# Two weight units ahead of the first norm, the squares of x behind them, and 10 idle products instead of 14

## The chip, the cores and the metric

The kernel runs on one core of a Trainium2 chip. The metric is the device time of one execution in microseconds (us). Three runs of the kernel before took 877.97, 880.21 and 880.77 us, so the median is 880.21 us.

## The reference, cut to what matters

One layer of a hybrid trunk on x of shape (1, 512, 1024), in float32. An RMS norm of x feeds one wide projection; its columns go to four token mixers (gated DeltaNet, RG-LRU, S5, RWKV-7) and to four gates; the gated branches are summed, projected and added to x, and a squared-ReLU MLP and a last norm follow.

```python
h = _rmsnorm(x, norm1_g)        # x * rsqrt(mean(x*x) + EPS) * g
proj = h @ w_in
p_gdn, p_lru, p_s5, p_rwkv, p_gate = _split(proj, ...)
ys = (gdn(p_gdn), rglru(p_lru), s5(p_s5), rwkv7(p_rwkv))
merged = sum(sigmoid(gate_i) * (ys[i] @ w_branch[i]))
x = x + merged @ w_out
x = x + square(relu(_rmsnorm(x, norm2_g) @ mlp_w1)) @ mlp_w2
```

## The kernel before, in words

Everything is held transposed: channels on the 128 partitions, the 512 tokens along the free axis. x comes as eight tiles `xs[0..7]` of 128x512 (L251).

**Units.** The weights come as 134 units of 128x1024 floats. `unit` (L316) asks for one: a DMA into one of four `raw` buffers (L313), on ACT a copy that rounds it to the high part `hi` (through the helper `act`, L117), on DVE a subtraction that leaves the low part `lo` (through `tt`, L120). There are two pairs of hi/lo buffers, so the high part of unit n waits until TensorE (PE) has finished unit n-2. A product of a unit is 24 matmuls of 128x512 (`gemm`, L337: eight blocks k, and in each hi by high, hi by low, lo by high part of x); "products" below means such matmuls.

**The first norm.** `norm1` (L406) does two things. `split_g` (L382) makes the high part (ACT, L117) and low part (DVE, L129) of each x tile, scaled by the norm's weight. `norm_stat` (L345) squares each tile on ACT, adds the squares on DVE (L120), lets PE sum them over the partitions (tile `ssa`), takes root and reciprocal (`sta`), and spreads the result with four matmuls (`rsa`) into the row `rs`. The projection runs on the unscaled x, and each result is multiplied by `rs` afterwards (`nproj`, L419), so PE does not need `rs` to start, but no result of the projection leaves PSUM before it is there. The first six accumulators have a PSUM bank each (EARLY = 6).

**What sets the order.** The program is written step by step (PLAN, L68), but the instructions are put in order by a list scheduler: each has a priority (`unit` gives -50000 to unit 0 and 100*u - 30000 to unit u, steps get levels by LV), and among those that its own timeline takes to be ready, the one of the best priority goes next on its engine. An engine then runs its list strictly in order. A change at the start shifts what is ready when, and so the order of everything in the mixers behind it.

**The triangular solve.** `tri_inverse` (L442), run for RWKV ("r") and for DeltaNet ("g"), is a chain over all engines: DMAs through a DRAM scratch (`scrr`, `scrg`; L446, L450), fifteen small steps on DVE, DMAs back and forth again (L466, L470), then bursts of tiny matmuls `zp` (128), `t1p` (192), `z2p` and `z3p` (64 each), with copies on ACT and DVE between them (L492, L507, L509, L519). "zpr" is the first burst for RWKV, "t1pr" the second, and so on; "zpg" that for DeltaNet.

**The S5 output.** `s5_y` (L1325) copies two PSUM tiles on ACT (L1335), writes them to DRAM (`scy`, L1338, from SP's queue), reads them back by 16 small DMAs issued from ACT's queue (L1344), adds on DVE (L129), applies Gelu on ACT, and multiplies by a weight on PE (`glu`).

The idle products are matmuls of a column of ones at the very start (`warm`, WARM of them; each is two instructions on PE).

Of the kernel before, what the change touches and what calls it, by code (L numbers as in the profile page):

```python
# [11 lines left out]
ACT = mybir.ActivationFunctionType  # L12
# [39 lines left out]
    sqc2=c3:236 sqc3=c3:16 sqc4=c3:533 sqc5=c3:610 sqc6=c3:562 sqc7=c3:594 rsc=c3:0  # L52
""".split())}
NU = 134
WARM = 14
EARLY = 6
GRAN = 32
DEEP = 2
# [39 lines left out]
RW0 = 1800  # L98
GATE0 = 2824
@with_exitstack  # L100
def trunk(ctx, tc, order, xT, wall, w8, prm, big, cst, gfr, out):
    nc = tc.nc
    V, A, G, P = nc.vector, nc.scalar, nc.gpsimd, nc.tensor
# [9 lines left out]
    def mm(o, l, r, start=True, stop=True):  # L113
        P.matmul(out=o, lhsT=l, rhs=r, start=start, stop=stop)  # L114

    def act(o, i, f, scale=1.0, bias=0.0):
        A.activation(out=o, in_=i, func=f, scale=scale, bias=bias)  # L117

    def tt(e, o, a, b, op):
        e.tensor_tensor(out=o, in0=a, in1=b, op=op)  # L120
# [44 lines left out]
    def fr(*ts_):  # L165
        clock[0] += 1
        for t in ts_:
            _, r, o, g, nm = live.pop(id(t))
            regions[r][1][o:o + g] = False
            regions[r][2][o:o + g] = clock[0]  # L170
# [10 lines left out]
    def t2(name, dt=F, where=None):  # L181
        return al(name, 512, dt, where)
# [10 lines left out]
    @contextmanager  # L193
    def priority(n):
        old = tc.cur_priority
        tc.cur_priority = n
        yield
        tc.cur_priority = old
# [14 lines left out]
    def ps(name):  # L213
        t = bank[0]
        turn[t] = (turn.get(t, -1) + 1) % BANKS[t]
        return pmx.tile([128, 512], F, tag=f"{t}{turn[t]}", name=name)
# [3 lines left out]
    def pa(name):  # L220

        n = turn["acc"] = turn.get("acc", -1) + 1
        if n < EARLY or turn.get("late"):
            b = n % 6
            if b >= 3:
                return pmx.tile([128, 512], F, tag=("g0", "g1", "s0")[b - 3], name=name)
            return pacc.tile([128, 512], F, tag=f"acc{b}", name=name)
        return pacc.tile([128, 512], F, tag=f"acc{n % 3}", name=name)


    def v3(t, a):
        return t.rearrange("p (a b) -> p a b", a=a)
# [4 lines left out]
    def bc(ap, shape):  # L237
        return ap.to_broadcast(shape)
# [7 lines left out]
    xs = [v3(xt, 8)[:, k] for k in range(8)]  # L246
# [44 lines left out]
    with priority(-70000):  # L291
        o = ps("warm")
        for i in range(WARM):
            mm(o[:, 0:128], ones, ones)
# [4 lines left out]


    count = {"u": 0, "raw": 0}
    third = []

    def place(key):
        if key not in order:
            order.append(key)
        return order.index(key)

    def load(key):
        n = count["raw"]  # L310
        count["raw"] += 1
        raw = wp.tile([128, 1024], F, tag=f"raw{n % NRAW}", name=f"raw{n}")
        nc.sync.dma_start(out=raw, in_=wall[place(key)])  # L313
        return raw

    def unit(key, more=None, chain=None):  # L316

        u = count["u"]
        count["u"] += 1
        with priority(100 * u - (30000 if u else 50000)):  # L320
            k = u % (DEEP + len(third) // 2)
            if k < DEEP:
                hi, lo = (wp.tile([128, 1024], R, tag=f"{e}{k}", name=f"{e}{u}") for e in ("hi", "lo"))
            else:
                hi, lo = third
            if chain is None:
                raw = load(key)
            else:
                raw = chain
                (G if more is None else nc.sync).dma_start(out=raw, in_=wall[place(key)], **({"accum_op": ADD} if more is None else {}))  # L330
            if more is not None:
                G.dma_start(out=raw, in_=wall[place(more)], accum_op=ADD)
            act(hi, raw, ACT.Copy)
            tt(V, lo, raw, hi.bitcast(F), SUB)
        return v3(hi, 8), v3(lo, 8)

    def gemm(o, w, rh, rl, nk=8, k0=0, first=True, last=True):  # L337
        wh, wl = w
        n = 0
        for k in range(nk):  # L340
            for a, b in ((wh, rh), (wh, rl), (wl, rh)):
                mm(o, a[:, k0 + k, :], b[:, k, :], first and n == 0, last and n == 3 * nk - 1)
                n += 1

    def norm_stat(xt, nm, parts=1):  # L345

        accs = []
        for k in range(8):
            sq = t2(f"sq{nm}{k}")
            act(sq, xt[k], ACT.Square)  # L350
            if k == 0 or k == 7:
                accs.append(sq)
            else:
                tt(V, accs[-1], accs[-1], sq, ADD)
                fr(sq)
        while len(accs) > parts:
            tt(V, accs[-2], accs[-2], accs[-1], ADD)
            fr(accs.pop())
        def keep_warm(n, t):
            if parts > 1:  # L360
                w = pa("warm")
                for _ in range(n):
                    mm(w[:, 0:128], ones, t[:, 0:128])

        o = ps("ss" + nm)
        for i, acc in enumerate(accs):
            for u in range(4):
                mm(o[:, u:u + 1], acc[:, u * 128:u * 128 + 128], one, i + u == 0, i == parts - 1 and u == 3)
            keep_warm(3, acc)
        fr(*accs)  # L370
        st = sm_.tile([128, 4], F, name="st" + nm)
        act(st, o[:, 0:4], ACT.Sqrt, 1.0 / 1024, eps_c)
        V.reciprocal(out=st, in_=st)
        rs = t2("rs" + nm)
        for h in range(2):
            o = ps("rs" + nm)
            for u in range(2):
                mm(o[:, u * 128:u * 128 + 128], bc(st[:, 2 * h + u:2 * h + u + 1], [128, 128]), ident)
            A.copy(out=rs[:, h * 256:h * 256 + 256], in_=o[:, 0:256])
        return rs  # L380

    def split_g(x, gname, k, hi, lo):  # L382

        act(hi, x, ACT.Copy, p(gname, k))
        stt(lo, x, p(gname, k), hi.bitcast(F), MUL, SUB)
# [17 lines left out]
    xgh, xgl = v3(xgh_, 8), v3(xgl_, 8)  # L403
    N1 = {}

    def norm1():  # L406

        for k in range(8):
            split_g(xs[k], "g1", k, xgh[:, k, :], xgl[:, k, :])
        N1["rs"] = norm_stat(xs, "a")  # L410
        fr(xt)

    def proj(col):

        o = pa("acc")
        gemm(o, unit(("in", col)), xgh, xgl)
        return o

    def nproj(t, col):  # L419
        tt(V, t, proj(col), N1["rs"], MUL)  # L420
        return t
# [851 lines left out]
    def s5_b():  # L1273
        b8 = S5["b8"]
        b83 = v3(b8, 16)

        up = t4("s5u")
        upv = up.rearrange("p (m t n) -> p m t n", m=2, t=8)
        scu = dram.tile([2, 128, 512], F, name="scu")
        for m in range(2):  # L1280
            tt(V, upv[:, m].rearrange("p t n -> p n t"), v3(proj(1544 + 128 * m), 64), v3(N1["rs"], 64), MUL)
            nc.sync.dma_start(out=scu[m], in_=up[:, m * 512:m * 512 + 512])
        ug = t4("s5ug")
        uf = scu.rearrange("m (g c) (t n) -> t c (m g) n", c=16, t=8)
        for t in range(8):
            nc.scalar.dma_start(out=v3(ug, 16)[16 * (7 - t):16 * (7 - t) + 16], in_=uf[t])
        ug3 = v3(ug, 16)
        H = t4("s5h")

        for r in range(2):  # L1290
            o = ps("s5v")
            for g in range(16):
                r0 = 64 * (g % 2)
                mm(o[r0:r0 + 64, (g // 2) * 64:(g // 2) * 64 + 64], b83[:, g, 64 * r:64 * r + 64], ug3[:, g, :])
            A.copy(out=H[:, 512 * r:512 * r + 512], in_=o)
        fr(b8)
        S5.update(up=up, ug=ug, H=H)
# [379 lines left out]
    def y_of(i, f):  # L1677
# [3 lines left out]

    steps = {
        "norm_a": norm1, "reg_y": lambda: region("c1a", 4096, R), "s5_a": s5_a, "s5_o": s5_o, "s5_b": s5_b, "s5_c": s5_c, "s5_y": y_of(2, s5_y), "lru_a": lru, "lru_g": y_of(1, lru_g),
        "rwkv_t": lambda: tri_prepare("r"), "rwkv_a": rwkv_a, "rwkv_b": rwkv_b, "rwkv_i": rwkv_i, "rwkv_r": rwkv_r, "rwkv_o": y_of(3, rwkv_o),
        "gdn_t": lambda: tri_prepare("g"), "gdn_k": lambda: gdn_a("k"), "gdn_v": lambda: gdn_a("v"), "gdn_q": lambda: gdn_a("q"), "gdn_l": gdn_logits, "gdn_b": gdn_b, "gdn_i": gdn_i, "gdn_r": gdn_r, "gdn_z": gdn_z, "gdn_c": y_of(0, gdn_c),
# [143 lines left out]
```

## Time and profile before

| | |
|---|---|
| median of three runs | 880.21 us |
| the profiled execution, its own time | 878.37 us |
| its span from first to last instruction | 876.6 us |
| PE busy | 852.6 us (97%) |
| DVE, ACT busy | 547.4 us, 427.2 us |
| mean granted TensorE clock | 0.988 |
| PE's idle time before 26 us | 0.89 at the very start, then some 3 us |
| PE's idle time from 150 to 335 us | some 12 us in 12 waits |
| PE's idle time from 350 to 800 us | 0.33 us |

PE is the engine that is nearly always busy. The first table of the page gives each engine's share of the span; the waits of PE, asked for by engine, say where the other 3% go; the timeline of the first 26 us shows the three engines step by step. "Busy" for PE includes the time in which it runs at half of its clock, which the granted clock of short windows shows.

### The profile page before, as it was taken

To read this page: it belongs to the slowest core of one execution; us is meant where nothing else is said; L and a number is where in the kernel's file an instruction comes from. 1 tells how busy PE (TensorE), PEld (TensorE's weight loads), DVE (VectorE), ACT (ScalarE), POOL (GpSimd) and SP (SyncE) were. 2 spreads that over 40 slices of the span, in tenths; PEclk is the share of its full clock that TensorE was granted. 3 is DMA by queue.
4 is the path that set the end of the run, shared out by engine and by line. 5 is a ranking of instruction groups with operands and counts; after the bars stand their busy time and mean duration, and the time that the engine had idled before them with its cause. 6 is when DMAs were issued, how large, how long until landed. Compare 5 with 4: busy or idle time off the path is not lost.

```text
span 876.6 us, 13021 instructions
## 1 busy us (share of the span) xinstructions
PE 852.6 (97%) x5175; PEld 683.9 (78%) x5175; DVE 547.4 (62%) x974; ACT 427.2 (49%) x600; POOL 26.0 (3%) x38
## 2 busy tenths in 40 slices
PE   8999999998999899999999999999999999999996
PEld 6777777777767677777888788888888888888885
DVE  6899796993676347845645652454437553868553
ACT  8735557954532254433523333765545443644433
POOL 1000000000000000000000000000100110010000
PEclk9999999998999899999999999999999999999998
DMA  8433345455365643344232232556676877463302
GB/s 298 134 114 104 109 117 111 105 148 147 111 182 155 163 144 111 107 119 136 73 106 99 75 130 96 192 145 174 164 195 165 239 170 194 164 137 104 120 25 96
DMA packets 79293, 119.97 MB, mean 137 GB/s; under 512 B 42544, under 2 KB 49392, under 8 KB 79216
## 3 DMA queue, kind: packets, MB, share of 16 engines
q1 hardware_dynamic: 51968, 100.40, 35.5%
q0 software_dynamic: 3456, 12.58, 8.5%
q10 hardware_dynamic: 23808, 6.16, 3.3%
q8 instruction: 40, 0.66, 0.3%
q14 instruction: 21, 0.17, 0.1%
HBM read 103.79 MB, written 13.17 MB: 133 GB/s over the span
## 4 chain that ended last, share of the span: by engine, by line
PE 80%; DVE 7%; DMA 6%; ACT 4%; issue 2%; ACTq 1%; SPq 1%; DVEq 0%
PE acc L114 24%; PE facc L114 20%; PE dacc L114 17%; PE oacc L114 5%; PE bacc L114 5%; DVE c L120 2%; DMA c1a<-scrg 1%; ACT c L117 1%; DVE lo L120 1%; PE s L114 1%; DVE c1a L120 1%; DVE c L129 1%; ACT L117 1%; DMA c1a<-gscr 1%; DMA scrg<-c1a 1%
## 5 line engine op out<-in xcount | busy, mean ns | idle before, releaser
L114 PE MATMUL acc<-c,hi 128*128 128x512 f32 x864 | 279.1, 401 | 3.1 <-DVE c L129 2.5
L117 ACT ACTIVATE hi<-raw 128x1024 fp32r<-128x1024 f32 x113 | 119.5, 1058 | 214.8 <-PE facc L114 73.5
L120 DVE TENSOR_TENSOR lo<-raw,hi 128x1024 fp32r<-128x1024 f32 x113 | 138.1, 1223 | 117.9 <-ACT hi L117 117.8
L114 PEld LDWEIGHTS acc<-c,hi 128*128 128x128 f32 x864 | 162.4, 191 | 43.2 <-DVE c L129 5.0
L114 PE MATMUL acc<-c,lo 128*128 128x512 f32 x432 | 175.1, 406 | 2.0 <-DVE lo L120 2.0
L114 PE MATMUL facc<-c,hi 128*128 128x512 f32 x336 | 103.4, 389 | 0.0
L114 PEld LDWEIGHTS acc<-c,lo 128*128 128x128 f32 x432 | 82.3, 190 | 21.9 <-DVE lo L120 3.1
L117 ACT ACTIVATE c<-c 128x512 f32<-128x512 f32 (+5 forms) x101 | 63.9, 638 | 19.3 <-DVE c L120 12.3
L114 PEld LDWEIGHTS facc<-c,hi 128*128 128x128 f32 x336 | 63.1, 188 | 13.0
L120 DVE TENSOR_TENSOR c<-c 128x16 f32<-128x16 f32 (+8 forms) x125 | 65.3, 537 | 5.1 <-ACT c L117 4.6
L114 PE MATMUL facc<-c,lo 128*128 128x512 f32 x168 | 65.5, 390 | 0.0
L114 PE MATMUL facc<-c,c1a 128*128 128x512 f32 x264 | 62.8, 391 | 0.0
L114 PE MATMUL dacc<-hi,c 128*128 128x512 f32 x176 | 57.4, 389 | 0.0
L117 ACT ACT_TABLE_LOAD x41 | 52.6, 1283 | 9.6 <-DMA c<-scu 3.7
L114 PEld LDWEIGHTS facc<-c,c1a 128*128 128x128 f32 x264 | 49.3, 188 | 10.2
L120 DVE TENSOR_TENSOR c1a<-raw,c1a 128x1024 fp32r<-128x1024 f32 x21 | 25.7, 1223 | 32.8 <-ACT c1a L117 32.7
L120 DVE TENSOR_TENSOR c<-acc,c 128x512 f32<-128x512 f32 x33 | 22.6, 688 | 36.3 <-PE acc L114 34.7
L114 PE MATMUL bacc<-c1a,hi 128*128 128x512 f32 x128 | 41.8, 408 | 0.3 <-DVE c L120 0.3
L117 ACT ACTIVATE c1a<-raw 128x1024 fp32r<-128x1024 f32 x21 | 22.2, 1059 | 36.6 <-PE facc L114 29.0
L114 PE MATMUL oacc<-c,hi 128*128 128x512 f32 x128 | 39.8, 392 | 0.1
L114 PEld LDWEIGHTS dacc<-hi,c 128*128 128x128 f32 x176 | 33.0, 188 | 6.9
L114 PEld LDWEIGHTS facc<-c,lo 128*128 128x128 f32 x168 | 31.5, 188 | 6.5
(394 smaller groups left out, 1187.2 us busy)
## 6 DMA issues: line engine op xcount, KB each, us to landing
raw<-in_wall_dram SPq DMA_DIRECT2D x134, 512.0 KB, 3.5
c<-in_wall_dram POOLq DMA_DIRECT2D x18, 512.0 KB, 5.8
c<-in_wall_dram SPq DMA_DIRECT2D x6, 512.0 KB, 3.5
raw<-in_wall_dram POOLq DMA_DIRECT2D x6, 512.0 KB, 6.2
scg<-c1b SPq DMA_DIRECT2D x11, 256.0 KB, 2.4
c<-scg SPq DMA_DIRECT2D x11, 256.0 KB, 4.2
c1b<-in_xT_dram SPq DMA_DIRECT2D x8, 256.0 KB, 5.4
c<-in_xT_dram SPq DMA_DIRECT2D x8, 256.0 KB, 4.8
```

The costliest lines, as they stand in the source:

```text
L114: P.matmul(out=o, lhsT=l, rhs=r, start=start, stop=stop)
L117: A.activation(out=o, in_=i, func=f, scale=scale, bias=bias)
L120: e.tensor_tensor(out=o, in0=a, in1=b, op=op)
L129: V.scalar_tensor_tensor(out=o, in0=a, scalar=s, in1=b, op0=op0, op1=op1)
```

## The change

The two first units of the projection (columns RW0 + 768 and RW0 + 896, which `rwkv_a` uses first) are asked for inside `norm1`, ahead of the splits, and kept in the list `early` until `proj` takes them. `unit` keeps the ACT instruction that makes each high part in the list `high`. All instructions of `norm_stat` on ACT are ordered behind `high[1]`, the high part of unit 1 (`tc.issue_after` adds an order edge on that instruction's engine alone). WARM goes from 14 to 10. The numbers of the units and their order in DRAM stay the same, and no work is added or left out but the four idle products.

```diff
-WARM = 14
+WARM = 10
...
-    third = []
+    third, high, early = [], [], []
...
-            act(hi, raw, ACT.Copy)
+            high.append(A.activation(out=hi, in_=raw, func=ACT.Copy, scale=1.0, bias=0.0).ins)
             tt(V, lo, raw, hi.bitcast(F), SUB)
...
     def norm1():
 
+        early.extend(unit(("in", RW0 + 128 * m)) for m in (6, 7))
         for k in range(8):
             split_g(xs[k], "g1", k, xgh[:, k, :], xgl[:, k, :])
-        N1["rs"] = norm_stat(xs, "a")
+        with tc.issue_after(high[1]):
+            N1["rs"] = norm_stat(xs, "a")
         fr(xt)
 
     def proj(col):
 
         o = pa("acc")
-        gemm(o, unit(("in", col)), xgh, xgl)
+        gemm(o, early.pop(0) if early else unit(("in", col)), xgh, xgl)
```

The order on ACT at the start. `c_75<-c1b,pr` is the high part of an x tile, `c_79<-c1b` (also c1a, c_78) its square, `hi_180`, `hi_214`, `hi_266` are the high parts of units 0, 1 and 2. Before, from the seventh x tile on (the six pairs ahead of these rows read the same):

```order
L117 ACTIVATE c_75<-c1b,pr 128x512
L117 ACTIVATE c_79<-c1b 128x512
L117 ACTIVATE c_75<-c1b,pr 128x512
L117 ACTIVATE c_78<-c1b 128x512
L117 ACTIVATE hi_214<-raw_216 128x1024
L117 ACTIVATE c_79<-cs,pr 128x128 x2
L117 ACTIVATE c_79<-pr 128x16
L117 ACTIVATE ea<-pr 128x4
L117 ACTIVATE cl<-pr 128x2
L117 ACTIVATE cl<-cl 128x2
L117 ACTIVATE hi_266<-raw_268 128x1024
```

Now, from the first instruction that works on data on, with units 0, 1, 2 as `hi_113`, `hi_119`, `hi_262`:

```order
L333 ACTIVATE hi_113<-raw_115 128x1024
L117 ACTIVATE c_75<-c1b,pr 128x512 x8
L333 ACTIVATE hi_119<-raw_121 128x1024
L117 ACTIVATE c_79<-c1b 128x512 x5
L117 ACTIVATE c1a<-c1b 128x512
L117 ACTIVATE c_79<-c1b 128x512
L117 ACTIVATE c_78<-c1b 128x512
L117 ACTIVATE c_79<-cs,pr 128x128 x2
L117 ACTIVATE c_79<-pr 128x16
L117 ACTIVATE ea<-pr 128x4
L117 ACTIVATE cl<-pr 128x2
L333 ACTIVATE hi_262<-raw_264 128x1024
```

The eight squares stood between the splits; they now stand in one block between the high parts of units 1 and 2. DVE follows: the low parts of x (L129) were alternating with the additions of squares (L120 of 128x512), and now come in one run of eight, then the low part of unit 1, then the additions.

The order on PE where the norm's sum over partitions (`ssa`) stands. Before, 26 products are ahead of it (24 of unit 0, two of unit 1):

```order
L114 MATMUL acc<-c_75,lo_181 128x512
L114 MATMUL ssa<-one,c_79 128x1 x4
L114 MATMUL acc<-c_75,hi_266 128x512 x2
L114 MATMUL acc<-c_75,lo_215 128x512
L114 MATMUL acc<-c_75,hi_214 128x512 x2
```

Now 50 products are ahead of it (units 0 and 1, two of unit 2):

```order
L114 MATMUL acc<-c_75,lo_120 128x512
L114 MATMUL acc<-c_75,hi_262 128x512 x2
L114 MATMUL ssa<-one,c_79 128x1 x4
L114 MATMUL acc<-c_75,hi_317 128x512 x2
L114 MATMUL acc<-c_75,lo_263 128x512
```

The matmuls of `rsa` move likewise, from behind 52 products to behind 77.

Far behind the start, the order on ACT where the copies of RWKV's solve meet the S5 output. Before, the four copies of `t1pr` and the copy of `z2pr` stand with no `scy` read near them; the 16 reads stand 15 rows further on:

```order
L495 COPY c_79<-c_78 32x16x16 x2
L117 ACTIVATE hi_2481<-raw_2483 128x1024
L691 COPY c_79<-c_79 64x256
L492 COPY c_78<-t1pr 16x16x16 x4
L117 ACT_TABLE_LOAD
L117 ACTIVATE c1a<-c1a 128x1024
L117 ACTIVATE hi_2515<-raw_2517 128x1024
L117 ACT_TABLE_LOAD
L117 ACTIVATE c1b<-c1b 128x512
L853 DMA c1a<-gscr 64x16x64
L509 COPY c1a<-z2pr 32x512
```

Now the reads of `scy` stand among these copies (the same lines of the program have numbers higher by two):

```order
L1346 DMA c_79<-scy 16x8x64
L494 COPY c_78<-t1pr 16x16x16
L1346 DMA c_79<-scy 16x8x64
L494 COPY c_78<-t1pr 16x16x16 x2
L693 COPY c_79<-c_79 64x256
L1346 DMA c_79<-scy 16x8x64 x2
L494 COPY c_78<-t1pr 16x16x16
L1346 DMA c_79<-scy 16x8x64 x7
L511 COPY c1a<-z2pr 32x512
L1346 DMA c_79<-scy 16x8x64 x3
L333 ACTIVATE hi_3078<-raw_3080 128x1024
L1346 DMA c_79<-scy 16x8x64 x2
```

On PE, 72 products stood between the end of zpr and the first of t1pr (30, 34 and 8 in three pieces), and now five; zpr itself moves from behind 496 products to behind 620, and zpg from behind 821 to behind 816.

## The prediction

> **What bounds the kernel now.** I read the page first: PE is busy nearly the whole span, so a change counts as far as it takes waits from PE, or adds some.
>
> ```profile
> span 876.6 us, 13021 instructions
> PE 852.6 (97%) x5175; PEld 683.9 (78%) x5175; DVE 547.4 (62%) x974; ACT 427.2 (49%) x600; POOL 26.0 (3%) x38
> ```
>
> Then the waits of PE by what it waited for (total, times, longest). The first row is the tiny matmuls of RWKV's solve, "issue" meaning that no semaphore explains it; the third is the start, where PE waits for the low parts of x.
>
> ```profile
> PE t1pr L114 <- issue: 2.9, 1, 2.9
> PE zpg L114 <- DMA c1a<-scrg: 2.6, 2, 1.4
> PE acc L114 <- DVE c L129: 2.5, 6, 0.8
> PE acc L114 <- DVE lo L120: 2.0, 3, 1.0
> PE glu L114 <- ACT c L117: 1.5, 1, 1.5
> ```
>
> Then stretches (length, busy time with instructions for PE, PEld, DVE, ACT, POOL, granted clock, DMA share, GB/s). From 8.1 to 16 us PE has 21 matmuls in 7.9 us and both DVE and ACT are busy all the time; in the late stretch nothing but PE counts.
>
> ```profile
> 8.10:16.00 7.90, 6.16 (x21) 3.43 (x21) 7.90 (x16) 7.90 (x14) 0.00 (x0) 1.00 1.04 403
> 500.00:600.00 100.00, 99.84 (x453) 82.11 (x454) 48.42 (x50) 53.41 (x75) 1.72 (x2) 1.00 0.45 142
> ```
>
> From the chain in order of time comes the pace of products: 96 in 21.76 us, 0.227 us each.
>
> ```profile
> 434.44 21.76 PE acc L114 x96
> ```
>
> The profiled execution took 878.37 us, 1.8 beyond its span and 1.8 below the median of 880.21; I make the sum as a difference and lay it on the median. About 0.3% (2.6 us) is what a measurement of this kernel can tell from no change.
>
> **The start, worked out.** These rows of the timeline (start, duration, engine) have the prices.
>
> ```profile
> 0.89 5.40 PE L114 MATMUL warm<-one 128*128 128x128 f32 x28 [0.89 <-POOL one L289]
> 5.09 1.06 ACT L117 ACTIVATE hi<-raw 128x1024 fp32r<-128x1024 f32 x1 [3.07 <-DMA raw<-in_wall_dram]
> 6.05 0.71 ACT L117 ACTIVATE c<-c1b,pr 128x512 fp32r<-128x512 f32 x1
> 6.67 0.62 ACT L117 ACTIVATE c<-c1b 128x512 f32<-128x512 f32 x1
> 7.32 1.41 DVE L129 SCALAR_TENSOR_TENSOR c<-c1b,pr,c 128x512 fp32r<-128x512 f32 x2
> 9.91 0.69 DVE L120 TENSOR_TENSOR c<-c 128x512 f32<-128x512 f32 x1
> 16.07 0.68 ACT L117 ACTIVATE c<-cs,pr 128x128 f32<-128x128 f32 x2
> 17.06 1.22 DVE L120 TENSOR_TENSOR lo<-raw,hi 128x1024 fp32r<-128x1024 f32 x1
> 17.22 1.06 ACT L117 ACTIVATE hi<-raw 128x1024 fp32r<-128x1024 f32 x1
> 17.26 1.00 PE L114 MATMUL ssa<-one,c 128*128 128x1 f32 x8
> 24.38 1.05 PE L114 MATMUL rsa<-cs,sta 128*128 128x128 f32 x8
> 25.19 0.48 PE L114 MATMUL acc<-c,hi 128*128 128x512 f32 x1
> ```
>
> Before, DVE pays a low part (0.70) and an addition (0.69) per x tile, and PE, which needs 3 x 0.227 = 0.68, waits. By the order, at 25.19 PE has 52 products, ssa and rsa behind it; 25 more bring it to 77 at 25.19 + 25 x 0.227 = 30.9 us. The changed order has 77 products behind it when rsa is done, so that is the point to compare.
>
> Now: DVE's low parts follow at 0.66 to 0.70 from 7.32 on, the eighth is done at about 12.7, if the x tiles are there. The last tiles and unit 1's raw weights land (issue start, then time to landing):
>
> ```profile
> L251 SPq DMA_DIRECT2D c1b<-in_xT_dram x2: 381/420/458, 4.5 to 5.1; - x2
> DMA to landing us min/median/max: 5.9/6.0/6.0
> L313 SPq DMA_DIRECT2D raw<-in_wall_dram x1: 491/491/491, 5.7 to 5.7; - x1
> DMA to landing us min/median/max: 6.7/6.7/6.7
> ```
>
> The last x tile is there at 5.1 + 6.0 = 11.1, in time; unit 1's weights at 5.7 + 6.7 = 12.4. Their high part takes 1.06, so PE starts unit 1 at 13.5 and waits for its low part (1.22 more, 14.7): 0.8 lost. The other 22 products end at 19.8. On ACT the squares, 0.52 apart, run from 13.4 to 17.6; the small scalings behind them (16.07 to 17.22 before, 1.15) end at 18.8, unit 2's high part at 19.8: just in time. DVE's additions end at about 20.2, as two small ones wait for ACT. PE: two products of unit 2 to 20.25, ssa to 21.4, then unit 3's high part, which stands behind a small operation that waits for DVE, at 21.8; 27 products to 27.9, rsa to 28.8. That is 2.1 us before 30.9; I take a gain of 2.0. Bounds: if nothing waits behind 8.12, 76 x 0.227 + 2.05 gives 27.4, a gain of 3.5; with full durations in place of starts (0.71 and 0.62 on ACT, 0.74 on DVE) the waits for the high parts of units 2 and 3 come back, 0.7 and 0.5, and about 1.0 is left.
>
> Ten idle products at 5.40 / 28 = 0.19 an instruction end at 4.8 instead of 6.3; the first real product waits for ACT until 6.81 either way, so that edit is worth nothing while the clock stays up. SP's queue has the same first 20 DMAs, so no load moves there.
>
> **Behind the start.** `rs` comes some four us later, with 25 products done in the meantime, so PE's accumulators (six banks, 144 products) do not block. But the mixers' chains start later and the scheduler has laid them out anew. PE's waits stood at three places with DMAs; I look what stands there now. Around t1pr (PE timeline, then two stretches):
>
> ```profile
> 200.99 0.26 PE L114 MATMUL t1pr<-c,c1b 32*16 32x16 f32 x9 [2.89 <-issue]
> 202.30 0.77 PE L114 MATMUL acc<-c,hi 128*128 128x512 f32 x1
> 206.62 0.39 PE L114 MATMUL acc<-c,lo 128*128 128x512 f32 x1
> ```
>
> ```profile
> 200.00:201.00 1.00, 0.01 (x2) 0.01 (x2) 0.00 (x0) 0.00 (x0) 0.00 (x0) 0.50 1.18 260
> 207.00:208.00 1.00, 1.00 (x6) 0.80 (x5) 0.69 (x1) 0.99 (x2) 0.00 (x0) 1.00 0.00 0
> ```
>
> The clock falls to half during the wait; the ten products from 202.30 to 206.62 take 4.32 us instead of 2.27, so it costs 2.05 more. With the 1.50 at glu, this place costs 2.89 + 2.05 + 1.50 = 6.4 us.
>
> In the changed order ACT issues the reads of scy among the copies of t1pr and z2pr. Prices, from ACT's timeline, SP's line and the page:
>
> ```profile
> 201.55 0.36 ACT L492 COPY c<-t1pr 16x256 f32<-16x256 f32 x1 [6.71 <-PE t1pr L114]
> 206.47 1.28 ACT L117 ACT_TABLE_LOAD   x1 [2.48 <-DMA c1a<-gscr]
> 211.09 0.63 ACT L117 ACTIVATE c1b<-c1b 128x512 f32<-128x512 f32 x1
> 211.74 0.58 ACT L509 COPY c1a<-z2pr 32x512 f32<-32x512 f32 x1
> 225.25 0.59 ACT L1335 COPY c<-s5y 128x512 f32<-128x512 f32 x1
> 230.99 2.72 ACTq L1344 DMA_DIRECT2D c<-scy  x6
> 240.44 1.06 ACT L117 ACTIVATE c<-c 128x1024 f32<-128x1024 f32 x1
> ```
>
> ```profile
> L1338 SPq DMA_DIRECT2D scy<-c x1: 320/320/320, 225.9 to 225.9; - x1
> DMA to landing us min/median/max: 2.6/2.6/2.6
> ```
>
> Counted from the end of zpr: ACT has the copy of zpr (0.5), a table load (1.28), an activation (0.63) and the second copy of s5y (0.59), then the write is issued and lands 2.6 later, so the first read goes out at about 5.8. Eleven reads at 0.46 (2.72 / 6), five small copies of 0.36 and its own 0.58 later z2pr is copied, at 13.4. PE has some S5 matmuls and five products (1.7), the t1pr burst (1.4), 20 products and two transposes (4.9), z2pr (1.0, after a wait of 0.9 for DVE's additions, which alternate with ACT's delayed copies), two bursts for DeltaNet and four products (2.7): 12.6, so it waits 0.8. DVE's copy of the other half stands behind an addition that needs the first eight reads landed: 1.2 more. Gelu stands on ACT behind five more reads (2.3), a high part (1.06), two other DMAs (1.2), three table loads (3.8) and two activations (1.7), and ends at 24.6; PE, with 24 products behind z3pr, is at glu at 21.7: 2.9. Together 0.9 + 0.8 + 1.2 + 2.9 = 5.8 where 6.4 went. If the clock stays up this is -0.6; if the wait of 2.9 halves it as the 2.89 did, +1.4. I take +0.4. [...]
>
> zpg waited 2.6 for scrg, and its DVE steps stand in the same place against the units' low parts; it now stands behind 816 products instead of 821, so it waits 5 x 0.227 = 1.1 longer (0 to 2). The waits for lo (2.0) I leave as they are.
>
> Sum: -2.0 + 0.4 + 1.1 = -0.5 us, so 879.7.
>
> **The rivals.** *Faster: the wait at t1pr goes.* It is no semaphore's; the tiny matmuls ran beside a DMA share over 1. If the new order feeds them, 2.89 and 2.05 go and half of the new ACT waits (2.9) comes: -2.0 - 6.4 + 2.9 = -5.5, 874.7. For it: the row says "issue", so no dependence asks for it. Against: bursts and DMAs stand closer together now.
>
> *Slower: ACT's queue at scy becomes the bound.* The 2.89 and the half clock stay, and the new waits of 5.8 replace only glu's 1.5: +4.3; with zpg's 1.1 and the start's -2.0 this is +3.4, and with the clock halved once more +5.5: 883.6 to 885.7, say 884.6. It decides once the first read of scy goes out over 4 us after zpr's end, which the landing time of 2.6 nearly ensures; against it, the t1pr wait was an accident of this order.
>
> *No gain at the start: unit 0 at half clock.* Half clock makes a product 0.43, three 1.3 against DVE's 0.66 to 0.70: eight tiles lose up to 4.9, of which unit 1's wait hides 0.8. With the other terms the time is 880.5 (0.8 lost) to 883.8. [...] The granted clock reads 1.00 in all early stretches of this trace, which speaks against it.
>
> **How the numbers follow.** The forecast gets 0.40, all within 0.3%. The faster rival gets 0.33. The slower gets 0.20. The cold start gets 0.07, of which 0.02 lies within 0.3%. So faster 0.33, same 0.42, slower 0.25. The range runs from below the faster rival, with its ACT waits gone too (-8.4, 871.8; I cut at 872.5), to the upper end of the slower, 885.7: 872.5 to 885.7.
>
> **What would show it.** Right: the eighth low part of x done before 13.2, PE at unit 1 by 13.6, rsa's last at 28.2 to 29.8 with 77 products behind. ACT's first scy read between t1pr copies, and waits of PE at z3pr and glu of 0.5 to 3 us each. Wrong: PE's pace in unit 0 at 0.43 (cold); waits of `acc` for hi beyond 1 us before 25 us; no wait at z3pr or glu; a wait for issue again at zpr or t1pr with a clock of 0.50 behind it (slower), or none and less than 9 us of PE waits from 150 to 335 (faster).

## The result, and the profile after

The changed kernel takes 873.74 us (median of 6 runs, 872.16 to 877.04), the kernel before beside it 880.36 (6 runs, 875.73 to 881.57): a ratio of 0.994, with a 95% interval of 0.9918 to 0.9962, so 6.6 us faster. The forecast was 879.7 with a range of 872.5 to 885.7. The time lies in the range, but near the faster rival's 874.7, not near the forecast.

The profiled execution was the longest of the six (877.04), so its trace shows less of the gain than the median. Its page:

```profile
span 875.2 us, 13000 instructions
PE 854.5 (98%) x5167; PEld 688.8 (79%) x5167; DVE 548.5 (63%) x974; ACT 424.6 (49%) x598; POOL 26.0 (3%) x38
```

The waits of PE (total, times, longest). The wait for `issue` at t1pr is gone from this list, one of 1.8 at `r` has come; zpg's went from 2.6 to 0.5, glu's from 1.5 to 0.2. zpr, which had no row before, now has 1.7, and bacc went from 0.3 to 2.2. us waits as before: 1.1 and 0.6 then, 1.7 and 0.2 now.

```profile
PE bacc L114 <- DVE c L120: 2.2, 1, 2.2
PE r L114 <- issue: 1.8, 1, 1.8
PE us L114 <- DVE c1b L691: 1.7, 1, 1.7
PE zpr L114 <- DMA c<-scrr: 1.7, 1, 1.7
PE acc L114 <- DVE lo L120: 1.5, 3, 0.7
...
PE zpg L114 <- DMA c1a<-scrg: 0.5, 1, 0.5
PE glu L114 <- ACT c L117: 0.2, 1, 0.2
```

PE's timeline of the start (start, duration, then the idle time before it and who ended it). Unit 0's products are long: two in 1.05 instead of 0.62. From 8.6 to 13.7 they are 0.43 apart, the pace of the ten products behind t1pr before (4.32 us, at a granted clock of 0.50); behind it they are 0.23 apart. By this pace alone I call it half clock at the start, here and in the experiments. The product behind `rsa`, with 77 products done, is at 29.84. In the kernel before the product behind the 77th starts at 30.98 (30.9 by the prediction's sum). Before:

```profile
30.98 0.39 PE L114 MATMUL acc<-c,lo 128*128 128x512 f32 x1
```

The changed kernel:

```profile
0.89 4.64 PE L114 MATMUL warm<-one 128*128 128x128 f32 x20 [0.89 <-POOL one L289]
...
6.67 0.80 PE L114 MATMUL acc<-c,hi 128*128 128x512 f32 x1 [1.15 <-ACT c L117]
...
12.85 1.05 PE L114 MATMUL acc<-c,hi 128*128 128x512 f32 x2
...
13.99 0.63 PE L114 MATMUL acc<-c,hi 128*128 128x512 f32 x2
...
29.03 1.05 PE L114 MATMUL rsa<-cs,sta 128*128 128x128 f32 x8
29.84 0.48 PE L114 MATMUL acc<-c,lo 128*128 128x512 f32 x1
```

Two later marks have the same work behind them in both orders (counted in PE's list): the last `ktT`, behind 480 products, and the first `xT`, behind 1536. Before:

```profile
166.23 0.60 PE L823 MATMUL ktT<-cs,c 128*128 128x128 f32 x4
...
500.05 0.33 PE L1447 MATMUL xT<-cs,c 128*128 128x128 f32 x1 [0.33 <-DVE c L120]
```

After:

```profile
163.56 0.38 PE L825 MATMUL ktT<-cs,c 128*128 128x128 f32 x2
...
498.72 0.33 PE L1449 MATMUL xT<-cs,c 128*128 128x128 f32 x1 [0.33 <-DVE c L120]
```

The `ktT` transposes are some 0.1 apart, so the last one starts at 166.56 before and 163.67 after. That cuts both spans into four stretches:

| stretch | before | after |
|---|---|---|
| start, to 77 products and `rsa` done | 31.0 | 29.8 |
| to the last `ktT` | 135.6 | 133.8 |
| to the first `xT` (the mixers) | 333.5 | 335.1 |
| to the end | 376.5 | 376.5 |

The first two give 2.9 us. The mixers' stretch, on which most of the prediction's working went, was no faster in this execution; but it is also the one that varies from execution to execution. The experiments ask what it is worth, and why.

### The profile page after: what moved, and what is told of

Same layout as the page of the kernel before. It is cut to its first block, busy times and chain, and to the rows that moved or that the text cites. A ratio compares the mean times of both kernels' runs of the same rounds, so it can differ in the third digit from the quotient of the medians.

```text
span 875.2 us, 13000 instructions
## 1 busy us (share of the span) xinstructions
PE 854.5 (98%) x5167; PEld 688.8 (79%) x5167; DVE 548.5 (63%) x974; ACT 424.6 (49%) x598; POOL 26.0 (3%) x38
## 4 chain that ended last, share of the span: by engine, by line
PE 83%; DVE 6%; DMA 5%; ACT 4%; issue 1%; SPq 0%; ACTq 0%; DVEq 0%
PE acc L114 27%; PE facc L114 20%; PE dacc L114 17%; PE oacc L114 5%; PE bacc L114 5%; DVE c L120 2%; DMA c1a<-scrg 1%; PE s5y L114 1%; DVE lo L120 1%; DMA scg<-c 1%; PE s L114 1%; ACT L117 1%; DVE c L129 1%; DVE c1b L120 1%; ACT hi L333 1%
## 5 line engine op out<-in xcount | busy, mean ns | idle before, releaser
L120 DVE TENSOR_TENSOR lo<-raw,hi 128x1024 fp32r<-128x1024 f32 x113 | 138.0, 1222 | 105.0 <-ACT hi L333 101.7
L114 PE MATMUL acc<-c,lo 128*128 128x512 f32 x432 | 172.6, 401 | 1.6 <-DVE lo L120 1.5
L120 DVE TENSOR_TENSOR c<-c 128x16 f32<-128x16 f32 (+8 forms) x125 | 65.1, 534 | 6.8 <-ACT c L117 5.3
L114 PEld LDWEIGHTS facc<-c,c1a 128*128 128x128 f32 x264 | 49.4, 188 | 10.1
L120 DVE TENSOR_TENSOR c1a<-raw,c1a 128x1024 fp32r<-128x1024 f32 x21 | 25.7, 1223 | 32.7 <-ACT c1a L333 32.6
L120 DVE TENSOR_TENSOR c<-acc,c 128x512 f32<-128x512 f32 x33 | 22.6, 689 | 36.5 <-PE acc L114 33.1
```

## The experiments

Times below are medians, "before" always the runs of the kernel before on the same chip. "Lost to the half clock" is span x (1 - mean granted clock): for the kernel before 12.3 us (29 runs).

### e1: the changed kernel again

> The changed kernel once more, for its times and for a second trace. Theory A (start and layout): about 874 again, of which the start gives 1.0 when unit 0 runs at half clock, as in the first trace of it, and 2 to 3.5 when it does not; the rest, 3 to 5, is gone from PE's waits and half clock between 150 and 335 us. Theory B (start alone): the whole 6.6 is there when rsa is done. Theory C (cold start): this trace shows unit 0 at a pace of 0.43 again. If it shows 0.227 instead, the pace differs between executions of one kernel, and the row for 77 products and rsa should read about 28.8 instead of 29.8.

872.69 us (6 runs, 871.62 to 873.51) against 879.46 (29 runs); ratio 0.9921, 0.9898 to 0.9944. In this trace the products of unit 0 are 0.43 apart only from 8.85 to 10.56, and 0.23 apart from 11.33 on; the product behind `rsa` is at 28.76. The mixers' stretch takes 330.8 instead of 335.1. So the start alone (Theory B) is not the whole: only 2.2 of 6.8 us are there when `rsa` is done. Unit 0 at half clock is real by its pace (Theory C), and its size differs between the two executions (until 13.7 there, until some 11 here).

```profile
28.76 0.48 PE L114 MATMUL acc<-c,lo 128*128 128x512 f32 x1
```

### e2: ten idle products, the order of before

```diff
-WARM = 14
+WARM = 10
```

> The kernel before with 10 idle products instead of 14 and nothing else; the order of all other instructions is that of before. Theory A and my sum: no difference (within 0.3%, 879 to 882), as PE waits for the low parts of x in unit 0 anyway. Theory C: unit 0 at half clock costs here less than in the changed kernel, since a low part and an addition on DVE (1.39) cover three products at half clock (1.3): 0 to 1 slower. A rival says that the four idle products are themselves on the path: 0.8 faster.

880.41 us (12 runs) against 879.46; ratio 0.9995, 0.9966 to 1.0023: no difference, as my sum had it, although the products of unit 0 are at half clock here too, until 11.8: the product behind the 77th starts at 30.97 as before. But its wait for `issue` is not quite at the place where before had it:

```profile
201.18 0.24 PE L114 MATMUL t1pr<-c,c1b 32*16 32x16 f32 x5 [2.70 <-issue]
```

Before, 172 of the 192 matmuls of t1pr stand ahead of the wait of 2.89; here 180 of them. Four idle products are eight matmul instructions (each of them is two: `warm` is x28 for fourteen and x20 for ten). The wait came eight matmuls later in the burst, so at the same number of the list.

### e3 and e4: the new order with 14 and with 20 idle products

```diff
-WARM = 10
+WARM = 14
```

> The changed kernel with 14 idle products, so the new order alone. Theory A: 873 to 875, as the changed kernel. Theory C: unit 0 runs at full clock, the row for 77 products and rsa reads about 28.8 instead of 29.8, and the time is 1 to 3 below that of the changed kernel on this chip. If unit 0 is still at half clock with 14, the count of idle products is not what decides.

> The changed kernel with 20 idle products (40 instructions), which end at about 8.6 at the pace of 0.19 and so run into unit 0's first products. Theory A: 0 to 2 slower than with 10 or 14, as the first real products start up to 1.8 later. Theory C: the clock is up for all of unit 0; three products per x tile take 0.68 and PE catches up with the splits on DVE by the eighth tile, so the time is 1 to 3 below that with 10.

With 14: 875.38 us (12 runs, 870.77 to 880.85; ratio 0.9958, 0.9935 to 0.998). With 20: 877.70 (12 runs, 872.67 to 881.02; ratio 0.9969, 0.9947 to 0.999). Both are slower than with 10, although the start is faster. Theory C had the faster start, but a shorter time with it, and that did not come. With 14 idle products no product of unit 0 has the pace of half clock, and the product behind `rsa` is at 28.19:

```profile
27.39 1.05 PE L114 MATMUL rsa<-cs,sta 128*128 128x128 f32 x8
28.19 0.48 PE L114 MATMUL acc<-c,lo 128*128 128x512 f32 x1
```

So ten idle products cost 0.6 us at the start by these two traces (28.76 against 28.19), and gain more than that somewhere behind it. None of the theories had that.

### e5 and e6: is it chance?

> The changed kernel a third time, beside e6 on one chip, to see whether ten idle products really beat fourteen by the 2.7 us of the first comparison (872.69 against 875.38). By the traces so far the stretches of equal work are the same in both (84th to 480th product 133.8 us, from the first xT on 376.5), the start is 0.6 to 1.6 longer with ten, and only the stretch from the 480th product to the first xT varies between executions, from 330.8 to 340.5, by how many half-clock windows of 1.7 us lost each it holds. Theory L (lottery): that stretch has the same spread in both, so the ten's lead was chance, and this time the two medians lie within 1.5 us of each other, ten about 873 to 876. Theory W (ten idle products change something in the mixers): ten is again 2 to 3.5 us ahead and again within 2 us from run to run.

> The changed order with fourteen idle products again. Theory L: within 1.5 us of e5, times spread over some 8 us or more as before (870.8 to 880.9). Theory W: 875 to 876.5, that is 2 to 3.5 us above e5.

Ten: 872.43 us (6 runs, 869.06 to 874.16). Fourteen: 875.68 (12 runs, 873.66 to 882.37), against 879.22 before (25 runs). The lead of ten is 3.2 us this time, after 2.7: chance does not explain it. Theory W holds, but for the narrow spread that it named (5.1 us this time), and it has to name what four idle products at the start change in the mixers. e6's trace has these waits (a product right behind t1pr, and t1pg):

```profile
217.34 0.72 PE L114 MATMUL acc<-c,hi 128*128 128x512 f32 x2 [1.86 <-issue]
...
298.49 0.23 PE L114 MATMUL t1pg<-c,c1a 32*16 32x16 f32 x4 [2.07 <-issue]
```

The changed kernel has none at t1pr, and at the other place one eight matmuls later in the list, where three of eight matmuls of `r` have been done:

```profile
301.76 0.34 PE L114 MATMUL r<-c,c 128*64 128x64 f32 x5 [1.82 <-issue]
```

I counted how many matmuls stand ahead of each such wait in PE's list:

| kernel | the wait stands behind | matmuls ahead of it |
|---|---|---|
| before | 172 of t1pr | 1240 |
| e2, order of before, 10 idle | 180 of t1pr | 1240 |
| e6, new order, 14 idle | all of t1pr and vtT | 1366 |
| e4, new order, 20 idle | 184 of t1pr | 1366 |
| changed kernel, 10 idle | 3 of an `r` within t1pg | 2250 |
| e6, new order, 14 idle | 154 of t1pg | 2251 |

The order, the time and the DMAs differ between these, the number hardly does. The waits for `issue` in the other traces fit: 1237 and 2250 in e8, 1238 and 2251 in e7, 1238, 1366 and 2251 in e3 (whose three waits are 0.55, 1.59 and 1.11). The page has a DMA queue of the kind "instruction":

```profile
q8 instruction: 40, 0.66, 0.3%
```

40 packets of 0.66 MB / 40 = 16.5 KB for 5175 matmuls and as many weight loads: some 130 matmuls a packet, and 1240 and 1366 are 126 apart, one packet. In the trace of before the only packet of that queue between 192 and 202 us starts in this half microsecond (198.0 to 198.5; packets, MB, share), just when PE runs dry; PE goes on at 200.99, some 2.7 us later. This holds for all 21 waits for `issue` above 0.3 us in the fourteen traces: PE goes on 2.2 to 2.75 us after a packet of that queue has started.

```profile
q8 instruction: 1, 0.02, 17.1%
```

By these counts and packets I read "issue" here as the wait for the next block of PE's instructions. 126 products take 126 x 0.227 = 28.6 us; from 500 to 800 us, where PE does little else, ten packets of that queue come in the trace of before and ten in that of the result, and PE has no wait for `issue` there. In the trace of before the 126 matmuls ahead of the 1240th, all of them tiny, are through in 1.4 us (196.71 to 198.10), and PE waits for the rest. Tiny matmuls alone do not make the wait: the block that ends at the 2250th matmul of before holds little else, and PE does not wait there. Its packet starts at 303.86, ahead of the burst, and PE is at that matmul 3.3 us later, at 307.19. So in these traces PE waits where it comes to a border earlier than 2.2 to 2.75 us behind the packet's start, and eight instructions at the very start moved the wait by eight matmuls (from 172 to 180 of t1pr, e2). The longest wait for `issue` of a trace is 2.9 us in the one of before, 2.7 in e2, 1.3 to 2.6 in the three of the changed kernel, and 4.0 in e8.

### e7 and e8: other orders

Four, or two, of the eight squares are queued behind unit 1's high part; the rest stay where they were before.

```diff
-        with tc.issue_after(high[1]):
-            N1["rs"] = norm_stat(xs, "a")
+        N1["rs"] = norm_stat(xs, "a")
...
-            act(sq, xt[k], ACT.Square)
+            if nm == "a" and k >= 4:
+                with tc.issue_after(high[1]):
+                    act(sq, xt[k], ACT.Square)
+            else:
+                act(sq, xt[k], ACT.Square)
```

> The squares of the first four x tiles stay between the splits as before the change, those of the last four are queued behind unit 1's high part; ten idle products. The order is a third one, in the start and in the mixers. Theory A (the start gives its share whatever the mixers do): four of eight tiles still cost DVE 1.39 instead of 0.70, so about half of the start's gain is left, 0.5 to 1.5 us by the row behind rsa (85 products ahead of it here; 32.7 in the order before, 31.2 to 32.2 here). The mixers' stretch from the 480th product to the first xT is a new layout and may lie 3 us to either side of before (333 to 339): time 874 to 882. Theory B (all of the gain is the start's): 876 to 878.

> As e7, but only the squares of the last two x tiles are queued behind unit 1's high part: a fourth order. Theory A: the start gives a quarter, 0 to 0.8 us (rsa has 75 products ahead of it here; its row would read 30.4 in the order before), and the mixers again what their new layout gives, 874 to 883. Theory B: 878 to 880, between before and e7.

e7 takes 883.82 us (12 runs; ratio 1.0054, 1.0037 to 1.0071), e8 885.93 (8 runs; 1.0079, 1.005 to 1.0108): slower than before by 4.6 and 6.7, although e7's start is 1.4 ahead of before (its product behind `rsa`, with 85 done, is at 31.44, where before has 32.8). e7 loses 22.3 us to the half clock and e8 21.1, where before loses 11.7 on that chip. In e7 the loss begins with a wait for `issue` behind all of t1pr, at the 1238th matmul by my count:

```profile
198.76 1.12 PE L114 MATMUL s5y<-c 128*128 128x64 f32 x5 [1.76 <-issue]
```

In e8 the wait stands one matmul earlier in the list and is the longest of all; its trace is at half clock from 202.2 to 229.5:

```profile
204.34 1.98 PE L114 MATMUL s5y<-c 128*128 128x64 f32 x9 [3.98 <-issue]
```

Stretches of e7 (length, busy PE with its matmuls, granted clock, DMA share, GB/s) show how it goes on. The first holds 197 matmuls, nearly all tiny; the clock is at half from 197.52 on and stays there for seven stretches of 3.42 us, with PE busy all the time behind the wait:

```profile
194.10:197.52 3.42, 2.90 (x197) 1.00 0.20 74
197.52:200.93 3.41, 2.17 (x11) 0.50 0.02 5
200.93:204.30 3.37, 3.37 (x18) 0.50 0.22 78
...
218.00:221.40 3.40, 3.40 (x12) 0.50 0.00 0
221.40:224.80 3.40, 3.40 (x16) 1.00 0.38 154
```

Both expectations were too kind: these two orders lose some 10 us more to the half clock than before does.

### e9: the border alone

```diff
         for i in range(WARM):
             mm(o[:, 0:128], ones, ones)
+        for i in range(4):
+            mm(o[0:32, 128:144], ones[0:16, 0:32], ones[0:16, 0:16])
```

> The changed kernel (ten idle products) with four tiny products of 16 rows by 16 columns behind them: eight matmul instructions more in PE's list, as fourteen idle products have, but only some 0.1 to 0.2 us of work. In all traces so far PE's waits for issue stand at the same places of its list, whatever the order: at about the 1240th, 1367th and 2250th matmul, and the profile counts 40 packets of 16 KB on the instruction queue for some 5170 matmuls, 128 to a packet with their weight loads. Theory F (instruction fetch): the wait comes where a whole packet is tiny matmuls. So here a wait of 1.2 to 2 us comes back right behind the t1pr burst (at about the 1367th) and the one near 2250 moves eight matmuls forward in the burst, to the place that it has with fourteen; time 875 to 877. Theory T (the time of the idle products, and the clock at the start, decide): 872 to 873.5, and no wait for issue at t1pr, as with ten.

876.90 us (12 runs, 871.52 to 881.56) against 879.86 (29 runs); ratio 0.9974, 0.9951 to 0.9997. Eight instructions (0.5 to 1.0 us in all, as `warm` takes 5.17 instead of 4.16 and 4.64, in a stretch in which PE waits anyway) take back 3.8 of the changed kernel's 6.8 us by the medians, and its narrow spread with them. The start is that of ten idle products (product behind `rsa` at 29.65). The waits are back at the two places of e6; the first is small in this execution, which was at half clock there (208 to 221; the two products behind the wait take 1.22 us, where they take 0.72 in e6), so PE, by my estimate from these two, came to the border later:

```profile
216.28 1.22 PE L114 MATMUL acc<-c,hi 128*128 128x512 f32 x2 [0.34 <-issue]
...
303.42 0.22 PE L114 MATMUL t1pg<-c,c1a 32*16 32x16 f32 x4 [0.80 <-issue]
```

Theory F holds, Theory T falls: what counts is the number of instructions, not the idle work.

### e10 and e12: moving the border away

```diff
+        for i in range(45):
+            mm(o[0:32, 128:144], ones[0:16, 0:32], ones[0:16, 0:16])
```

e10 is the kernel before with 10 idle products and these 45 tiny ones, e12 is e7 with 42 of them.

> The kernel before, its order untouched, with 10 idle products and 45 tiny ones (16 rows by 16 columns) behind them: 82 matmul instructions more in PE's list than before, some 1 to 2 us of work in a stretch in which PE waits anyway. Theory F: the 1240th matmul now lies in the middle of the 192 of t1pr instead of near their end, so that no packet holds only tiny ones: the wait for issue of 2.8 at t1pr and the half clock right behind it (3.4 of lost time, 198 to 206) are gone, a wait of 1 to 2 for issue may come at t1pg instead; time 873 to 877. Theory T: no gain; 879 to 882, and the wait at t1pr stays.

> The order of e7 (883.8; it loses 22 us to the half clock, most of it in one stretch from 197 to 221 us that begins at a wait for issue of 1.76) with 42 tiny products of 16 rows by 16 columns behind the ten idle ones: 84 matmul instructions more in the list. Theory F: the packet that was all tiny matmuls is split, the wait goes, and with it the stretch at half clock that begins there; lost time 10 to 14 instead of 22, time 870 to 875. If only the wait goes and the clock falls all the same because so many tiny matmuls stand together: 880 to 883. Theory T: 883 to 886, no change.

e10: 877.98 us (12 runs) against 879.86, ratio 0.9988, 0.9966 to 1.001: not told apart from no change. The wait of 2.8 at t1pr is gone, as expected; what remains for `issue` is this, one block behind the 2250th matmul:

```profile
310.65 0.18 PE L114 MATMUL t1pg<-c1a,c 32*32 32x16 f32 x1 [1.12 <-issue]
```

But its trace has a half clock of 6.8 us at 105 to 112, where no other trace has one, and waits of 2.0 and 1.5 for scrg at zpg. What was won at t1pr was lost in other places. That a wait for `issue` can be moved by tiny instructions is shown; that this pays is not, for this order. The wait that is left stands behind 2379 matmuls.

e12: 879.17 us (12 runs; ratio 0.9996, 0.9979 to 1.0013) where e7 took 883.82. The loss to the half clock fell from 22.3 to 14.5, the wait of 1.76 became 0.32, so 4.6 us came back with nothing but 84 instructions more. The 0.32 stands behind 1112 matmuls, one block ahead of the 1240th. The rest of the expected 10 did not: its trace has a new wait of 5.45 for an addition on DVE at `vtT` (219.72), which e7 does not have. What makes it is not shown.

### e11: seven wide idle products

Seven idle products of 256 columns are as much idle work as fourteen of 128, in six instructions fewer than ten.

```diff
-WARM = 10
+WARM = 7
...
-            mm(o[:, 0:128], ones, ones)
+            mm(o[:, 0:256], ones, bc(one, [128, 256]))
```

> The changed kernel with seven idle products of 256 columns in place of ten of 128: as much idle work as fourteen narrow ones (it should end at about 6.3 instead of 5.1), in six matmul instructions fewer than ten have. Theory F: no wait for issue at t1pr, as with ten, and the one near the 2250th matmul stays at 1 to 2.6 (six matmuls later in the list, in the last 34 of t1pg); the start is that of fourteen (the row behind rsa at 28.2 to 28.8 instead of 28.8 to 30.3, no half clock in unit 0), so 0.5 to 1.5 below the changed kernel's 872.4 to 873.7: 871 to 872.5, with little spread. Theory T (more idle work is what makes fourteen slower): 875 to 876.

870.50 us (5 runs, 869.84 to 872.36) against 880.03 (8 runs); ratio 0.9897, 0.9876 to 0.9917. Its median is the lowest of all, 2 to 3 us below the changed kernel's three; the intervals of the ratios overlap, so the size of this lead is open. The idle work ends at 6.80, unit 0 is at full clock, the product behind `rsa` is at 28.39, there is no wait for `issue` at t1pr, and the other is at the 2250th matmul again:

```profile
0.89 5.91 PE L114 MATMUL warm<-one 128*128 128x256 f32 x14 [0.89 <-POOL one L289]
...
28.39 0.48 PE L114 MATMUL acc<-c,lo 128*128 128x512 f32 x1
...
295.34 0.17 PE L114 MATMUL t1pg<-c1a,c 32*32 32x16 f32 x1 [2.29 <-issue]
```

## Why the prediction was right and wrong

Where the 6.8 us of the changed kernel come from, by the medians of e1 and e5 and the stretches of the three traces of it: the start gives 1.4 (its product behind `rsa` at 29.84, 28.76 and 30.27, mean 29.6, against 31.0), the next stretch 1.8, the end nothing. So 3.6 are left for the mixers. With fourteen idle products the medians gain 4.1 and 3.5, the start 2.5 and the next stretch 1.8: nothing, or up to 0.8 lost, is left for the mixers. The new order by itself is worth nothing there; some 4 us go with the block borders, as e9 took 3.8 back with eight instructions. Of these 4 the waits for `issue` make 1.7 (1.8, 2.6 and 1.3 in the traces with ten, 3.3 and 3.9 with fourteen), and the half clock some 1 (10.5 to 11.3 lost, by the medians of all runs, against 11.8 and 12.2); where the rest lies is not shown. These shares of the medians are remainders: single traces of the mixers' stretch scatter (330.8, 331.8 and 335.1 with ten, 333.4 and 333.5 with fourteen, 340.5 with twenty, and in the order of before 333.5 and, in e2, 339.4).

**The start, -2.0: right in mechanism, and the order alone gives 2.2 to 2.8.** The eighth low part of x was done at 13.3 (13.2 had been the mark) and 77 products were ahead of the one behind `rsa`. In the changed kernel 0.7 to 2.2 are left of it.

**"That edit is worth nothing while the clock stays up": the step that failed.** The clock did not stay up. The cold start, to which I gave 0.07 because the granted clock read 1.00 in all early stretches, was there in all three traces of the changed kernel and cost some 0.6 (e1 beside e3) and 1.5 us (e5 beside e6, 30.27 against 28.79). These are pairs of single traces, and the two with fourteen, without a cold start, differ by 0.6 themselves. The row that I leaned on doesn't show it: the trace of the result reads 1.00 there too, while its products are 0.43 apart. And the same edit moved every instruction of PE behind it by eight places, which gained some 4 us. I had priced four idle products by their time, and not as instructions.

**The place around t1pr, +0.4.** The wait of 2.89 went, as the faster rival said, but not because the new order feeds the burst better: with fourteen idle products that order waits 1.6 to 1.9 right behind the burst. The half clock did not go with it: it now begins while zpr runs, or at its end, and lasts 17.1, 6.8 and 10.2 us in the three traces of the changed kernel, where before has 6.8. In e1, with no wait in the first two stretches:

```profile
205.78:209.19 3.41, 3.41 (x17) 3.41 (x18) 1.92 (x2) 2.61 (x5) 0.00 (x0) 0.50 0.93 326
209.19:212.60 3.41, 3.41 (x56) 2.47 (x57) 2.73 (x6) 1.18 (x3) 0.00 (x0) 0.50 0.73 280
212.62:216.03 3.41, 3.41 (x169) 3.13 (x161) 2.08 (x6) 1.07 (x3) 0.00 (x0) 1.00 0.29 93
```

So the clock's fall does not hang on that wait. The price of the new ACT waits (0.9 + 0.8 + 1.2 + 2.9) was wrong: nothing at z2pr and z3pr, 0.2 to 0.7 at glu. The order was read rightly: in e1 the first scy read goes out between copies of t1pr, at 213.5, 7.9 behind zpr's end where I had 5.8, and the Gelu ends at 233.6, 27.9 behind it where I had 24.6. But PE came later still, at glu 27.4 behind zpr's end where I had 21.7: 18 of S5's matmuls between zpr and t1pr take 3.8 us there at half clock (2.1 in e3 at full), two bursts of `s1g` 1.0 each, and the 6.8 us at half clock from 205.8 on (3.4 lost) were not in my sum. The slower rival fell with the same step.

**zpg, +1.1: wrong in sign.** It waits 0.5 to 0.6 instead of 2.6 in the three traces. In exchange zpr waits 0.8 to 1.7 for scrr and bacc 1.5 to 2.4, where before has none and 0.3; us waits 1.3 to 1.7 for DVE and up to 0.4 for ACT, as much as before. PE's waits from 30 us to the first xT come to 10.1 and 9.7 (first trace, e1) against 12.0 before: the waits changed their places more than their sum.

**A stretch that I left out.** From `rsa` to the last `ktT` PE is 1.8 us faster, in every trace of the new order. 0.75 of it is a wait for a unit's low part (1.01 before, 0.26 after). The rest, 1.0, goes with other groupings of the small bursts among the products; I have not shown how.

So the time came out near the faster rival's 874.7, and that is in part luck. Of the rival's terms the wait at t1pr did go, but by the edit that I had costed at nothing; the half clock there (2.05) stayed, the ACT waits (2.9) did not come, and the stretch that I left out gave 1.8. The forecast of 879.7 failed by 6 us, and the range held only because it reached down to that rival.

## What to carry to other kernels

Where a row says `issue`, count how many instructions of that engine stand ahead of it, in two versions of the kernel. If the number is nearly the same, as here (1237 to 1240, 1366, 2250 and 2251), set it beside the packets of the queue "instruction" (126 to 130 matmuls each, here): an edit ahead of such a wait, even one that does no work, may move it into or out of a burst of tiny instructions, as the eight instructions of e9 did (3.8 us). An edit is to be priced in time, and in instructions; and a new order is to be compared over many runs and at marks with equal work behind them, since the loss to the half clock went with such edits too (22.3 us in e7, 14.5 in e12, which differ by 84 instructions).

## What the runs showed of the hardware

**In these traces the clock falls and rises on a grid of 3.41 us.** These three neighbouring stretches of the trace of before, cut on that grid, read exactly 0.50, 0.50, 1.00:

```profile
199.68:203.10 3.42, 2.11 (x26) 0.50 1.02 211
203.10:206.52 3.42, 3.42 (x9) 0.50 0.15 44
206.52:209.94 3.42, 3.42 (x20) 1.00 0.00 0
```

In the trace of the result the same holds for a stretch that stays at half for five grid steps, from 204.96 to 222.03:

```profile
201.55:204.96 3.41, 1.63 (x11) 1.00 1.36 217
204.96:208.38 3.42, 3.42 (x58) 0.50 1.13 269
...
218.60:222.03 3.43, 3.43 (x21) 0.50 0.54 163
222.03:225.40 3.37, 3.37 (x16) 1.00 0.39 96
```

The falls of one trace fit one grid (before: 199.68, 295.25 and 308.90, 28 and 4 steps of 3.413 apart), and its offset from the program's start differs from execution to execution, also of one kernel: 60 steps are 204.78, and the clock falls at 204.96 in the trace of the result and at 205.78 in e1. The half clock around t1pr lasted five, two and three steps (17.1, 6.8 and 10.2 us) in the three traces of the changed kernel, at 1.7 us lost a step. Such differences are much of the spread within one kernel: with fourteen idle products (e3) the fastest run, 870.8, has a mean granted clock of 0.993, so 6.1 us lost, and the slowest, 880.9, has 0.980, so 17.6 us lost. The clock fell behind a stretch with PE busy for 2.90 of 3.42 us, with 197 mostly tiny matmuls (e7), and stayed down through stretches in which PE was busy throughout (3.37 of 3.37 us, 3.40 of 3.40). What decides is not shown.
